# Batched matmul on one core: the small zeroing store beside the first loads writes 16 rows of 512 B instead of 128

## The chip, the cores and the metric

The kernel runs on one core of a Trainium2 chip (trn2). The metric is device microseconds of that core, as the median of several executions. Lower is better.

Engines in the profile: PE is TensorE (matmul), PEld its weight loads, DVE is VectorE, ACT is ScalarE, POOL is GpSimd, SP is SyncE. "SPq" and "ACTq" are the two queues on which this kernel starts DMAs. In this kernel SBUF holds the tiles of a, b and the output, PSUM is what the matmuls write to, and an eviction copies a result from PSUM to SBUF. "Packet records" are the lines that the packed trace keeps for each DMA packet: its start, duration, size and queue. They don't name the DMA engine, so a time "per engine" below is a sum divided by 16, unless the text says otherwise. In this kernel a data packet is one row (6144 packets of 8192 B for 48 full transfers of 128 rows). The records also hold 4-byte packets, 16 for each full transfer, here read as the semaphore writes that report completion, one for each engine that a transfer uses: each of the first four casts of before starts 0.36 to 0.43 us after the last of the 16 of its load. The load rows agree with 16 engines: 128 rows of 309 ns pass in 2.45 us, so 16 run at a time.

## The reference

```python
# batch 16, K = M = N = 512, float32
def reference(a, b):            # a: [16, 512, 512] (k, m), b: [16, 512, 512] (k, n)
    return np.matmul(a.transpose(0, 2, 1), b).astype(np.float32)
```

It reads 32 MiB and writes 16 MiB. That traffic sets most of the kernel's time, as the profile below shows.

## The kernel before

Each batch has two loads of 1 MiB (a and b), two casts to bf16 on DVE, 16 matmuls on PE, two evictions from PSUM on ACT and one store of 1 MiB. SP issues all loads and then all full stores. The output of every batch has its own SBUF tile, so no store has to make room for anything. A full load or store has 128 rows of 8192 B.

```python
    with tc.tile_critical(no_gpsimd_drain=True):
        def load(i):
            j = i % NL                                    # NL = 3 load buffers
            if i >= NL:
                nc.sync.wait_ge(s_acast, i - NL + 2)
            nc.sync.dma_start(a_ts[j][:], a_v[i]).then_inc(s_a[j], 16)
            nc.sync.dma_start(b_ts[j][:], b_v[i]).then_inc(s_b[j], 16)

        def store(i):
            if i == 0:
                nc.sync.wait_ge(s_w, 16)                  # the small store has landed
            nc.sync.wait_ge(s_ev1, i + 1)
            nc.sync.dma_start(out_v[i], o_ts[i][:]).then_inc(s_o, 16)

        for i in range(batch):
            load(i)
        for i in range(batch):
            store(i)
        nc.sync.wait_ge(s_o, 16 * batch)
        # ... DVE: wait for a, cast; wait for b, cast.  PE: 16 matmuls a batch (cut)

        nc.gpsimd.memset(o_ts[0][:, 0, 0:P], 0.0).then_inc(s_z, 1)
        nc.scalar.wait_ge(s_z, 1)
        nc.scalar.dma_start(out_v[0][:, 0, 0:P], o_ts[0][:, 0, 0:P]).then_inc(s_w, 16)
        nc.scalar.wait_ge(s_w, 16)
        for i in range(batch):
            for h in range(H):                            # H = 2
                nc.scalar.wait_ge(s_mm, H * i + h + 1)
                nc.scalar.copy(
                    out=o_ts[i][:, 2 * h:2 * h + 2, :], in_=ps_ts[(i % NB) * H + h][:]
                ).then_inc(s_ev1 if h else s_ev0, 1)
```

The last block is the subject. Before any matmul has finished, POOL zeroes 128 rows x 128 columns of the first output tile and ACT stores them. The full store of batch 0 overwrites the bytes later, so the result doesn't need this store. ACT waits for the store to land before its first eviction, because that eviction overwrites the tile that the store reads.

## Time and profile before

| | before |
|---|---|
| time, median of 3 | 125.76 us (125.68 to 125.79) |
| span of the profiled execution | 123.6 us |
| PE / DVE / ACT busy | 48% / 32% / 27% |
| DMA engines | 9 tenths or more in all but the first and last of 40 slices |

From the page of the kernel before: the DMA rows of the 40 slices (share of time the 16 DMA engines are busy, then GB/s), the packets, the two queues, and the issues with their time from issue to landing.

```profile
DMA  2999999999999999999999999999999999999993
GB/s 58 414 424 430 424 424 424 424 419 424 424 424 422 416 424 422 422 424 424 419 414 422 422 424 424 424 422 427 424 427 427 432 430 424 427 435 427 427 424 143
DMA packets 7056, 50.40 MB, mean 408 GB/s; under 512 B 784, under 2 KB 912, under 8 KB 912
...
q1 hardware_dynamic: 6912, 50.33, 97.6%
q10 hardware_dynamic: 144, 0.07, 0.2%
...
a<-in_a_dram SPq DMA_DIRECT2D x16, 1024.0 KB, 8.6
...
out_dram<-o ACTq DMA_DIRECT2D x1, 64.0 KB, 4.9
```

The 9s say that the DMA engines have work from the second slice to the last but one. This kernel ends when its DMA stream ends: from 100 to 118 us there is no compute at all, and the DMA share is 1.01. q1 is SP's queue, q10 ACT's: 144 packets, 128 rows and 16 semaphore writes. The 784 packets under 512 B are the 4-byte ones: 16 for each of 48 full transfers, and 16 for the small store, so by the reading above each DMA uses all 16 engines.

From the timeline of the kernel before (start us, duration us, engine, line, operation; in brackets the idle time before it and what ended it):

```profile
0.94 0.38 SPq L63 DMA_DIRECT2D a<-in_a_dram  x1
0.94 0.20 POOL L108 MEMSET o<- 128x128 f32 x1 [0.50 <-SPq L57]
1.18 0.37 ACTq L110 DMA_DIRECT2D out_dram<-o  x1
...
5.98 1.23 DVE L83 CAST abf<-a 128x2048 bf16<-128x2048 f32 x1 [5.98 <-DMA a<-in_a_dram]
8.51 1.23 DVE L85 CAST bbf<-b 128x2048 bf16<-128x2048 f32 x1 [1.31 <-DMA b<-in_b_dram]
11.01 1.23 DVE L83 CAST abf<-a 128x2048 bf16<-128x2048 f32 x1 [1.27 <-DMA a<-in_a_dram]
...
13.70 1.28 ACT L115 ACT_TABLE_LOAD   x1 [13.70 <-PE ps L97]
...
88.28 1.01 ACT L115 COPY o<-ps 128x1024 f32<-128x1024 f32 x1 [0.71 <-PE ps L97]
```

The casts start when their loads land, so their starts are a clock of the DMA stream. ACT's store is issued at 1.18 us and lands 4.9 us later, at about 6.1 us. ACT has nothing to do until 13.7 us anyway, and its release there comes from PE. The last eviction ends at 89.3 us; the remaining 34 us are stores draining.

### The profile page before, as it was taken

What the parts mean: (1) busy time and instruction counts of PE and PEld (TensorE: products, weight loads), DVE (VectorE), ACT (ScalarE), POOL (GpSimd) and SP (SyncE); (2) the same over time, 40 slices, a digit from 0 to 9 for tenths busy, and PEclk for the clock granted to TensorE, in tenths of its full rate; (3) what the DMA queues carried; (4) which work ended last, traced back from release to release, by engine and by line L of the source; (5) the groups of instructions that cost most, each with busy time, mean ns of one, the idle gap of its engine ahead of it and who ended that gap; (6) DMA issues with size and microseconds to landing.
All of it is one profiled execution on the core that took longest, in us unless ns stands there. A gap on an engine that the chain in (4) does not pass through costs nothing. (4 is left out here: it accounts for less than half of the span.)

```text
span 123.6 us, 750 instructions
## 1 busy us (share of the span) xinstructions
PE 59.6 (48%) x256; PEld 28.0 (23%) x256; DVE 39.3 (32%) x32; ACT 33.6 (27%) x33; POOL 0.4 (0%) x5
## 2 busy tenths in 40 slices
PE   0007979695865956859659578596500000000000
PEld 0002344252332522424325234243200000000000
DVE  0055345633554356435543464352000000000000
ACT  0000565623425336244263352432600000000000
POOL 1000000000000000000000000000000000000000
PEclk9999999999999999999999999999985555555555
DMA  2999999999999999999999999999999999999993
GB/s 58 414 424 430 424 424 424 424 419 424 424 424 422 416 424 422 422 424 424 419 414 422 422 424 424 424 422 427 424 427 427 432 430 424 427 435 427 427 424 143
DMA packets 7056, 50.40 MB, mean 408 GB/s; under 512 B 784, under 2 KB 912, under 8 KB 912
## 3 DMA queue, kind: packets, MB, share of 16 engines
q1 hardware_dynamic: 6912, 50.33, 97.6%
q10 hardware_dynamic: 144, 0.07, 0.2%
HBM read 33.55 MB, written 16.84 MB: 408 GB/s over the span
## 5 line engine op out<-in xcount | busy, mean ns | idle before, releaser
L97 PE MATMUL ps<-bbf,abf 128*128 128x512 bf16 x256 | 59.6, 387 | 28.7 <-PEq L94 28.7
L115 ACT COPY o<-ps 128x1024 f32<-128x1024 f32 x32 | 32.3, 1013 | 42.0 <-PE ps L97 42.0
L97 PEld LDWEIGHTS ps<-bbf,abf 128*128 128x128 bf16 x256 | 28.0, 114 | 59.8 <-issue 37.6
L83 DVE CAST abf<-a 128x2048 bf16<-128x2048 f32 x16 | 19.6, 1227 | 25.8 <-DMA a<-in_a_dram 25.8
L85 DVE CAST bbf<-b 128x2048 bf16<-128x2048 f32 x16 | 19.6, 1227 | 19.3 <-DMA b<-in_b_dram 19.3
L115 ACT ACT_TABLE_LOAD x1 | 1.3, 1283 | 13.7 <-PE ps L97 13.7
L108 POOL MEMSET o<- 128x128 f32 x1 | 0.2, 205 | 0.5 <-SPq L57 0.5
L132 POOL MEMSET const-bfloat16-1.0<- 128x1 bf16 x1 | 0.1, 102 | 0.0
L132 POOL MEMSET const-uint8-127<- 128x1 uint8 x1 | 0.1, 102 | 0.0
L132 POOL MEMSET const-float32-0.0<- 128x1 f32 x1 | 0.1, 99 | 0.2 <-issue 0.2
L132 POOL MEMSET const-float32-1.0<- 128x1 f32 x1 | 0.1, 99 | 0.0
## 6 DMA issues: line engine op xcount, KB each, us to landing
a<-in_a_dram SPq DMA_DIRECT2D x16, 1024.0 KB, 8.6
b<-in_b_dram SPq DMA_DIRECT2D x16, 1024.0 KB, 10.7
out_dram<-o SPq DMA_DIRECT2D x16, 1024.0 KB, 25.8
out_dram<-o ACTq DMA_DIRECT2D x1, 64.0 KB, 4.9
```

The lines of the kernel that those rows point to most:

```text
L83: nc.vector.tensor_copy(out=abf_ts[i % NB][:], in_=a_ts[i % NL][:]).then_inc(s_acast, 1)
L85: nc.vector.tensor_copy(out=bbf_ts[i % NB][:], in_=b_ts[i % NL][:]).then_inc(s_bcast, 1)
L97: mm = nc.tensor.matmul(ps_ts[u * H + mo // 2][:, mo % 2, :], a_m[:, ko, mo, :], bbf_ts[u][:, ko, :], start=(ko == 0), stop=(ko == KO - 1),)
L108: nc.gpsimd.memset(o_ts[0][:, 0, 0:P], 0.0).then_inc(s_z, 1)
L115: nc.scalar.copy(out=o_ts[i][:, 2 * h:2 * h + 2, :], in_=ps_ts[(i % NB) * H + h][:]).then_inc(s_ev1 if h else s_ev0, 1)
L132: nc = _bacc.Bacc("TRN2", target_bir_lowering=False, num_devices=1)
```

## The change

The intent is to make the small store smaller: one eighth of the rows.

```diff
-        nc.gpsimd.memset(o_ts[0][:, 0, 0:P], 0.0).then_inc(s_z, 1)
+        nc.gpsimd.memset(o_ts[0][0:16, 0, 0:P], 0.0).then_inc(s_z, 1)
         nc.scalar.wait_ge(s_z, 1)
-        nc.scalar.dma_start(out_v[0][:, 0, 0:P], o_ts[0][:, 0, 0:P]).then_inc(s_w, 16)
+        nc.scalar.dma_start(out_v[0][0:16, 0, 0:P], o_ts[0][0:16, 0, 0:P]).then_inc(s_w, 16)
         nc.scalar.wait_ge(s_w, 16)
```

## The prediction

> **What bounds the kernel.** The DMA engines. In the page's 40 slices the DMA row is at 9 tenths from the second slice to the last but one, at 414 to 435 GB/s. The queue table gives the SP queue, with all loads and all full stores (50.33 MB), 97.6% of the 16 engines' span of 123.6 us. PE is busy 48%, DVE 32%, ACT 27%. The chain of waits ends in the last eviction, at 89.3 us; after it run only stores queued long before: from 100 to 118 us there is no compute and DMA share 1.01. The SP queue's own waits (57.9 us for DVE's casts) don't matter: about two loads are always queued. So only DMA engine time, or the ramp of the first 3 us, can move the total.
>
> **What the change removes.** The zeroing store on the ACT queue goes from 128 rows of 512 B to 16. In the trace's packet records that queue has 128 data packets of 27 ns and 16 semaphore packets of 9 ns: 3.60 us of engine time, 0.225 us for each of the 16 engines (the 0.2% of the queue table). After: 16 x 27 + 16 x 9 = 0.58 us, 0.036 us each. Saved: 0.19 us per engine. [...] I expect one data packet per engine. The memset (0.20 us on POOL) shrinks too. The order of instructions is unchanged on every engine, and nothing is added.
>
> **How much is on the critical path.** Nearly all. [...] the small store's packets run 2.6 to 3.7 us after the first load packet, when the engines are already fed, and the first b lands 2.58 us after the first a where later loads are 2.45 us apart: 0.12 us more; the rest of the 0.22 us falls into the first a. Every later packet is shifted by it, to the end. ACT's wait for the small store (landing 4.9 us after issue, at about 6.1 us) costs nothing: ACT's first work starts at 13.7 us, released by PE.
>
> **Prediction.** 125.76 - 0.19 = 125.57 us, with 8 in 10 between 125.25 and 125.90. Faster by over 2%: 1%; within 2%: 98%; slower by over 2%: 1%.
>
> **What would show each step.** (1) ACT queue: 32 packets instead of 144, under 0.05% of the engines' span; 6944 packets in all. (2) The interval from first a to first b falls from 2.58 towards 2.46 us. (3) Casts, matmuls, evictions and stores start about 0.2 us earlier, with unchanged durations; first cast at about 5.85 instead of 5.98 us. (4) The span falls to about 123.4 us. (5) The small store's landing falls from 4.9 to about 4.2 us. (6) Load packets keep their mean (about 313 ns in mid-run, against 309 ns for stores).
>
> **What would make it wrong.** Load packets take 309 ns in the first 10 us and 313 ns between 20 and 80 us. If that depends on the engines' relative phase, and the small store sets that phase, the 4096 load packets could gain or lose up to about 4 ns each: 1.1 us in all, more than the saving and of either sign. If the small store mostly filled time in which the engines would have waited in the ramp, the gain would be nearer zero. Both stay far inside 2%.

The sum: 0.225 us per engine before, 0.036 us after, 0.19 us saved. 16 rows going to 16 engines, one data packet each: the 0.036 us rest on that, and the trace of before could not show it.

## The result, and the profile after

Ratios here are the mean time of one kernel's runs over that of the other's of the same rounds, so they are not quite the ratio of the medians that are quoted.

| | before | after |
|---|---|---|
| time, median of 6 | 125.78 us (125.68 to 125.85) | 125.57 us (125.50 to 125.61) |
| ratio to before, 95% interval | | 0.9983, [0.9970, 0.9996] |
| span of the profiled execution | 123.6 us | 123.5 us |

The change saves 0.21 us by the medians. The same lines of the page, after:

```profile
DMA  3999999999999999999999999999999999999993
GB/s 53 417 435 427 427 422 425 422 419 419 425 425 425 425 425 425 422 419 419 422 422 417 419 425 425 422 425 427 425 425 430 433 425 430 433 425 427 425 425 130
DMA packets 6944, 50.34 MB, mean 408 GB/s; under 512 B 784, under 2 KB 800, under 8 KB 800
...
q1 hardware_dynamic: 6912, 50.33, 97.8%
q10 hardware_dynamic: 32, 0.01, 0.0%
...
out_dram<-o ACTq DMA_DIRECT2D x1, 8.0 KB, 4.3
```

The DMA row has the same shape, 112 packets are gone, and the 784 packets under 512 B are still 784. In the packet records of after each of the 16 rows starts 3 to 4 ns before a load row ends, and a load row starts 23 to 24 ns after it, another one for each small row: 16 rows still use 16 engines. The timeline after:

```profile
0.95 0.19 POOL L108 MEMSET o<- 16x128 f32 x1 [0.50 <-SPq L57]
1.17 0.38 ACTq L110 DMA_DIRECT2D out_dram<-o  x1
...
5.80 1.23 DVE L83 CAST abf<-a 128x2048 bf16<-128x2048 f32 x1 [5.80 <-DMA a<-in_a_dram]
8.27 1.23 DVE L85 CAST bbf<-b 128x2048 bf16<-128x2048 f32 x1 [1.24 <-DMA b<-in_b_dram]
10.75 1.23 DVE L83 CAST abf<-a 128x2048 bf16<-128x2048 f32 x1 [1.25 <-DMA a<-in_a_dram]
...
88.00 1.01 ACT L115 COPY o<-ps 128x1024 f32<-128x1024 f32 x1 [0.71 <-PE ps L97]
```

The first cast starts 0.18 us earlier, the second 0.24 us, the third 0.26 us, and the last eviction 0.28 us. So the shift arises in the first two loads and is then carried along. In the packet records of the two traces the last packet of the SP queue ends 119.94 us after the first one before, and 119.74 us after the change: 0.19 us less. The spans differ by only about 0.1 us. One pair of profiles can't be read finer than that: the profiled execution of before was at 125.61 us itself one of the fastest of its kernel. The packet records also show how the 128 rows of before run: by their spacing, the first three of each engine's eight rows alternate with load rows (329 to 330 ns apart), and the other five come in one burst, 23 to 30 ns apart, between the last row of the first a and the first row of the first b. The interval from first a to first b, 2.58 us with them and 2.45 us without, shows the burst: 5 x 23.5 ns = 0.12 us.

### The profile page after: what moved, and what is told of

It reads as the page before. It is cut to its first block, busy times and chain, and to the rows that moved or that the text cites. A ratio compares the mean times of both kernels' runs of the same rounds, so it can differ in the third digit from the quotient of the medians.

```text
span 123.5 us, 750 instructions
## 1 busy us (share of the span) xinstructions
PE 60.3 (49%) x256; PEld 28.1 (23%) x256; DVE 39.3 (32%) x32; ACT 33.7 (27%) x33; POOL 0.4 (0%) x5
## 2 busy tenths in 40 slices
DMA packets 6944, 50.34 MB, mean 408 GB/s; under 512 B 784, under 2 KB 800, under 8 KB 800
## 5 line engine op out<-in xcount | busy, mean ns | idle before, releaser
L97 PE MATMUL ps<-bbf,abf 128*128 128x512 bf16 x256 | 60.3, 390 | 27.7 <-PEq L94 27.6
```

Source lines behind the costliest of these rows:

```text
L97: mm = nc.tensor.matmul(ps_ts[u * H + mo // 2][:, mo % 2, :], a_m[:, ko, mo, :], bbf_ts[u][:, ko, :], start=(ko == 0), stop=(ko == KO - 1),)
```

## The experiments

Theory A was the prediction's: the DMA engines are always busy, so each packet of the small store pushes the whole stream back by its own length. Rivals were a fixed cost per DMA (B), a useful phase of the engines (C), the release of ACT (D), and a cost that only the start-up has (E). Each kernel was timed in 5 rounds against before (4 to 6 executions of each). Twelve runs were made, all with the right result. "Difference" is the difference of the medians from before in the same rounds. The interval of each small ratio is about 0.0013 to either side, that is 0.16 us.

| run | what it has | time us | before us | ratio | difference us |
|---|---|---|---|---|---|
| e1_none | no small store | 125.47 | 125.82 | 0.9969 | -0.35 |
| e2_no_act_wait | 128 rows, ACT doesn't wait | 125.80 | 125.82 | 0.9999 | -0.02 |
| e3_mid_run | 128 rows, amid the loads | 125.59 | 125.82 | 0.9982 | -0.23 |
| e4_x8_128rows | 8 stores of 128 rows | 133.32 | 125.82 | 1.0569 | +7.50 |
| e5_127rows | 127 rows | 138.58 | 125.81 | 1.1016 | +12.77 |
| e6_wide | 128 rows of 2048 B | 126.33 | 125.81 | 1.0047 | +0.52 |
| e7_memset_full | store 16 rows, zero 128 | 125.45 | 125.81 | 0.9968 | -0.36 |
| e8_x8_16rows | 8 stores of 16 rows | 125.57 | 125.81 | 0.9981 | -0.24 |
| e9_x8_no_wait | as e4, ACT doesn't wait | 126.93 | 125.69 | 1.0095 | +1.24 |
| e10_127_no_wait | as e5, ACT doesn't wait | 128.11 | 125.69 | 1.0191 | +2.42 |
| e11_x8_mid | 8 stores of 128 rows, amid the loads | 126.52 | 125.69 | 1.0069 | +0.83 |
| e12_after_again | the changed kernel | 125.36 | 125.69 | 0.9974 | -0.33 |

### e1_none: no small store

```diff
-            if i == 0:
-                nc.sync.wait_ge(s_w, 16)
...
-        nc.gpsimd.memset(o_ts[0][:, 0, 0:P], 0.0).then_inc(s_z, 1)
-        nc.scalar.wait_ge(s_z, 1)
-        nc.scalar.dma_start(out_v[0][:, 0, 0:P], o_ts[0][:, 0, 0:P]).then_inc(s_w, 16)
-        nc.scalar.wait_ge(s_w, 16)
```

> No small store, no memset for it, no waits for it. Theory A (DMA engine time: every packet of the small store delays the saturated stream by its own length): 0.225 us below before, about 125.55 us, and only 0.036 us below the changed kernel. Rival B (the small store has a fixed cost as a DMA, beside its rows, that 16 rows still pay): clearly more than 0.225 us below before. Rival C (the small store sets a useful phase of the engines): no gain, or a loss, and load packets of another mean than 313.5 ns in mid-run.

It took 125.47 us, 0.35 us below before, interval of the ratio [0.9956, 0.9982]. The upper end is 0.23 us below before, about where theory A's 0.225 us stands, so the size is at the edge of what A allows. Rival C falls: there is a gain, and the load packets in mid-run have the same mean (313.5 ns) as in both kernels. Rival B is not settled by this run.

### e2_no_act_wait: all 128 rows, but ACT doesn't wait

```diff
+    z_t = pool.tile([P, P], f32, name="z0")
...
-        nc.gpsimd.memset(o_ts[0][:, 0, 0:P], 0.0).then_inc(s_z, 1)
+        nc.gpsimd.memset(z_t[:], 0.0).then_inc(s_z, 1)
         nc.scalar.wait_ge(s_z, 1)
-        nc.scalar.dma_start(out_v[0][:, 0, 0:P], o_ts[0][:, 0, 0:P]).then_inc(s_w, 16)
-        nc.scalar.wait_ge(s_w, 16)
+        nc.scalar.dma_start(out_v[0][:, 0, 0:P], z_t[:]).then_inc(s_w, 16)
```

> All 128 rows stay, but the source is a tile of its own and ACT no longer waits for the store; the wait before the first full store stays on SP. Theory A: same as before within 0.06 us, since the engines move the same packets. Rival D (the smaller store helped because ACT, or the compute behind it, is released earlier): near the changed kernel, about 0.2 us below before.

125.80 us, ratio 0.9999: nothing gained. With one small store ACT's wait is free, and rival D falls as an explanation of the change.

### e7_memset_full: half of the change alone

```diff
-        nc.gpsimd.memset(o_ts[0][0:16, 0, 0:P], 0.0).then_inc(s_z, 1)
+        nc.gpsimd.memset(o_ts[0][:, 0, 0:P], 0.0).then_inc(s_z, 1)
```

(against the changed kernel)

> The store of 16 rows as in the changed kernel, but the memset of all 128 rows as before: half of the change alone. Theory A: the time of the changed kernel, 0.19 to 0.2 us below before. If the memset carried any of the gain: nearer before.

125.45 us, 0.36 us below before. The whole gain is there without the smaller memset: the store's rows carry it.

### e12_after_again: the changed kernel once more

> The changed kernel once more, in the same rounds as these. It was 0.21 us below before; with the memset of all rows it was 0.36, with no store 0.35. If those differ only by noise: 0.2 to 0.36 below before, so 125.45 to 125.6. It shows how far such differences can be read.

125.36 us, 0.33 us below before. (The time is just under the expected 125.45 us because before itself was 0.12 us lower in these rounds than in the earlier ones; the difference lies in the expected range.) So three comparisons of a 16-row store with before gave 0.21, 0.36 and 0.33 us, mean 0.30 us. A difference of 0.1 us between two of these runs says nothing.

### e4_x8_128rows: eight stores at the start

```diff
-        nc.scalar.dma_start(out_v[0][:, 0, 0:P], o_ts[0][:, 0, 0:P]).then_inc(s_w, 16)
-        nc.scalar.wait_ge(s_w, 16)
+        for c in range(8):
+            nc.scalar.dma_start(
+                out_v[0][:, c // 4, (c % 4) * P:(c % 4 + 1) * P], o_ts[0][:, 0, 0:P]
+            ).then_inc(s_w, 16)
+        nc.scalar.wait_ge(s_w, 128)
```

(SP's wait before the first full store goes to 128 as well.)

> Eight small stores of 128 rows of 512 B at the start instead of one. Theory A: 7 x 0.225 = 1.58 us above before, about 127.35 us (1.25% slower), with 1152 packets of 3.6 us x 8 engine time on the ACT queue. A rival by which the rows only fill a gap of the ramp, or by which rows write in parallel with the loads' HBM reads (packets' durations overlap): clearly less, under 0.8 us.

It cost 7.50 us instead of 1.58. The page shows at once that this is another mechanism (DMA rows of the 40 slices of e4_x8_128rows):

```profile
DMA  3999999980399999999999999999999999999993
GB/s 52 416 421 423 421 418 421 421 354 0 85 429 424 424 434 419 424 421 416 429 421 424 419 421 426 419 426 421 421 436 429 424 424 436 424 426 429 429 426 140
```

The DMA engines, which never pause in before, stand still for more than a slice (a slice is 3.3 us). The waits of the same run (engine, line, who was waited for, us in total, times, longest) name who held them up:

```profile
DVE abf L83 <- PE ps L97: 14.1, 3, 11.9
ACT o L118 <- DMA out_dram<-o: 9.6, 1, 9.6
```

Neither line is among before's waits. ACT waits 9.6 us for the small stores before it evicts anything. PE then has no free PSUM (it starts again at 26.2 us, once the evictions have begun at 25.0), so DVE may not overwrite the bf16 tiles (the first line), so SP may not issue the next loads (it waits for a cast of a for up to 14.9 us, where before had 8.0), and the DMA queue runs dry. The small stores land so late (25.0 us from the start of the span) because their rows don't go first: in the packet records most 512 B rows come one load row apart (their 64 rows per engine are spread over 20 us).

### e5_127rows: one row less

```diff
-        nc.gpsimd.memset(o_ts[0][:, 0, 0:P], 0.0).then_inc(s_z, 1)
+        nc.gpsimd.memset(o_ts[0][0:127, 0, 0:P], 0.0).then_inc(s_z, 1)
         nc.scalar.wait_ge(s_z, 1)
-        nc.scalar.dma_start(out_v[0][:, 0, 0:P], o_ts[0][:, 0, 0:P]).then_inc(s_w, 16)
+        nc.scalar.dma_start(out_v[0][0:127, 0, 0:P], o_ts[0][0:127, 0, 0:P]).then_inc(s_w, 16)
```

> 127 rows instead of 128: one row less, 512 B less. [...] Theory A, read by the engine (the engine with the most work sets the end): 127 x 27 ns = 3.43 us on that one engine against 0.225 us, so about 3.2 us above before, 129.0 us (2.5% slower), and all 127 data packets run one after the other. If it is the bytes or the packets in all that count: the same as before within 0.05 us. If the later loads can be taken up by the 15 others: in between[...].

Two passages are cut: the reason given for all 127 rows going to one engine, and a claim about whether later loads could move to the other engines. No run had shown either by then, so the 3.2 us rested on an assumption of the author. This run shows the first; e10 shows one engine still at work 2.45 us after all others.

It cost 12.77 us. One row fewer makes the kernel 10% slower. Two lines of the page of e5_127rows, and one of its waits:

```profile
DMA  3999999900039999999999999999999999999993
...
DMA packets 7040, 50.40 MB, mean 369 GB/s; under 512 B 769, under 2 KB 896, under 8 KB 896
```

```profile
ACT o L115 <- DMA out_dram<-o: 15.6, 1, 15.6
```

769 packets under 512 B are the 768 of the full transfers and a single one for the small store: 127 rows ran on one engine. The stretch from 28 to 30 us, when the queued loads are through, agrees: its DMA share is 0.06, one engine of 16. In the packet records the 512 B rows come 329 to 330 ns apart for most of 26 us, which fits one load row of 309 ns before each. The exceptions are a burst of eight rows between the first a and the first b, and one row more at each later change from one load to the next. The store landed at 31.1 us, about 30 us after its issue (before's 128 rows took 4.9 us), and ACT's first eviction waited for it. My expectation had only the engine time in it. The run therefore mixes two effects, and so does e4; e9 and e10 take them apart.

### e9_x8_no_wait and e10_127_no_wait: the same stores without ACT's wait

Both store from a tile of their own, so ACT needs no wait. For eight stores:

```diff
+    z_t = pool.tile([P, P], f32, name="z0")
...
-        nc.gpsimd.memset(o_ts[0][:, 0, 0:P], 0.0).then_inc(s_z, 1)
+        nc.gpsimd.memset(z_t[:], 0.0).then_inc(s_z, 1)
         nc.scalar.wait_ge(s_z, 1)
-        nc.scalar.dma_start(out_v[0][:, 0, 0:P], o_ts[0][:, 0, 0:P]).then_inc(s_w, 16)
-        nc.scalar.wait_ge(s_w, 16)
+        for c in range(8):
+            nc.scalar.dma_start(
+                out_v[0][:, c // 4, (c % 4) * P:(c % 4 + 1) * P], z_t[:]
+            ).then_inc(s_w, 16)
```

(SP's wait before the first full store goes to 128.)

> Eight stores of 128 rows at the start as in the run that cost 7.5 us, but from a tile of their own and without ACT's wait for them, so that evictions never wait. Theory A' (engine time alone; a 512 B packet lengthens the stream by its start-to-start distance of 23.5 ns, which the records of the 127-row run show, and the rest of the 7.5 us was ACT waiting): 7 x 8 x 23.5 ns = 1.3 us, up to 1.6 us with 225 ns each, above before: 127.1 to 127.4 us, and no stretch with an idle DMA row. If the DMA engines themselves stall on many small writes: still some 7 us above before.

For 127 rows it is the edit of e2 with `z_t[0:127, :]`:

> 127 rows from a tile of its own, without ACT's wait. Theory A': the one engine that has all 127 packets gets 127 x 23.5 ns = 2.98 us more work, the others none, and the slowest engine sets the end: 2.98 - 0.19 = 2.8 us above before, about 128.6 us. If bytes in all count: 125.6 to 125.8 us. If the DMA stall of the earlier run was not ACT's wait: 12 us above before again.

Eight stores now cost 1.24 us, so ACT's wait was about 6.3 us of e4's 7.5. The 127 rows cost 2.42 us, so the wait was about 10.4 us of e5's 12.8. The small remainders are what theory A is about. Both came out below the 1.3 to 1.6 us and the 2.8 us that had been expected. In e9 no slice is idle any more, as expected (DMA row of e9_x8_no_wait):

```profile
DMA  4999999999999999999999999999999999999993
```

In e10 the end of the run shows one engine working alone (stretches of the trace from:to, length, busy time of the engines, granted clock, DMA share, GB/s):

```profile
120.00:121.00 1.00, 0.00 (x0) 0.00 (x0) 0.00 (x0) 0.00 (x0) 0.00 (x0) 0.50 1.00 426
121.00:122.00 1.00, 0.00 (x0) 0.00 (x0) 0.00 (x0) 0.00 (x0) 0.00 (x0) 0.50 0.39 164
122.00:123.00 1.00, 0.00 (x0) 0.00 (x0) 0.00 (x0) 0.00 (x0) 0.00 (x0) 0.50 0.08 33
123.00:124.00 1.00, 0.00 (x0) 0.00 (x0) 0.00 (x0) 0.00 (x0) 0.00 (x0) 0.50 0.06 25
```

A share of 0.06 is one engine of 16. Fifteen engines are done near 121.5 us, and the sixteenth, by inference the one that carried the rows, needs about 3 us more. In the packet records its last semaphore write comes 2.87 us after the mean of the other fifteen, and 2.45 us after the last of them: 127 rows of 23.5 ns would be 2.98 us. In before the engines end up to 0.37 us apart, and it is the slowest of them that the run is compared with; that may be part of why the run cost less than 2.8 us. So in this run the engine with the most work set the end, and the bytes in all did not.

### e3_mid_run and e11_x8_mid: the same rows later

e3 takes the block at the start away (as e1 does, but SP's wait stays) and adds after the evictions of batch 6:

```diff
+            if i == 6:
+                nc.scalar.wait_ge(s_ev1, 1)
+                nc.scalar.dma_start(out_v[0][:, 2, 0:P], o_ts[0][:, 2, 0:P]).then_inc(s_w, 16)
```

> The store of 128 rows of 512 B is taken from the start and issued by ACT after its evictions of batch 6, amid full loads, with finished values. Theory A: engine time costs the same anywhere in a saturated stretch, so same as before within 0.06 us. Rival E (the rows cost time because they sit in the start-up, where everything later waits for the first a and b): about the time of the changed kernel or less, 0.2 us below before.

125.59 us, 0.23 us below before, interval of the ratio [0.9969, 0.9995]. Theory A as stated had expected no difference, within 0.06 us. The interval excludes zero; its end, at 0.06 us below before, just touches what A had allowed. e11 magnifies it: one such store after each of the batches 4 to 11, writing the finished values of eight different pieces of the first output tile (SP waits for 128).

> Eight stores of 128 rows, one after each of the batches 4 to 11, nothing at the start. Theory A': the same as eight at the start without the wait, 127.1 to 127.4 us, 1.5 to 1.8 us above no store at all. If the time of rows in mid-run is partly free (as 125.59 us for one store in mid-run against 125.81 for it at the start hints), it is clearly less, by 0.1 us for each store: about 126.3 to 126.5 us. If it is the start-up alone that costs 0.2 us once, whatever the number: 0.2 us below eight at the start.

It took 126.52 us, 0.83 us above before. Against no store at all (0.35 us below before) eight stores in mid-run cost 1.18 us, 0.15 us each; eight at the start (e9) cost 1.59 us, 0.20 us each. So rows in mid-run are not free, but cheaper. The packet records show a refund: in e11 the load packets between which the rows come last 309.8 ns, where they last 313.5 ns otherwise. Summed over the 3840 load packets after the first 256, each engine's load packets took 0.48 us less than in e1_none, which is 0.06 us for each small store. In the start-up, once the ramp's first 2.6 us are over, load packets last 309 ns anyway. But e9 gets a refund too, later: in before the load packets lengthen to about 313 ns from about 15 us after the first packet on, in e9 they stay at 309.0 ns until about 32 us, some 10 us after its last small row. That makes 0.26 us per engine less than in e1_none, 0.03 us for each store. So the refund accounts for 0.22 us of the 0.41 us between e9 and e11, and the rest is not much more than the interval of one comparison. Why load packets have these two lengths, and what ends the short ones, no run shows.

### e8_x8_16rows: as many rows in eight issues

```diff
-        nc.scalar.dma_start(out_v[0][0:16, 0, 0:P], o_ts[0][0:16, 0, 0:P]).then_inc(s_w, 16)
-        nc.scalar.wait_ge(s_w, 16)
+        for c in range(8):
+            nc.scalar.dma_start(
+                out_v[0][0:16, c // 4, (c % 4) * P:(c % 4 + 1) * P], o_ts[0][0:16, 0, 0:P]
+            ).then_inc(s_w, 16)
+        nc.scalar.wait_ge(s_w, 128)
```

(against the changed kernel; SP waits for 128 too)

> Eight stores of 16 rows of 512 B: as many data packets as before's one store of 128 rows, but eight issues and 128 semaphore packets. Theory A: 8 x (27 + 9) = 0.288 us per engine, so 0.06 us above before and 0.25 us above the changed kernel. Rival B (each DMA has a fixed cost to the stream, beyond its packets): 7 x that cost above; with 0.1 us each, 0.7 us above before.

125.57 us, 0.24 us below before, where 0.06 us above had been expected. Rival B falls clearly, since eight issues cost no more than one. But the number of theory A is missed too: by packets e8 has slightly more engine time than before (4.61 us against 3.60 us on the ACT queue) and is yet faster. Two things differ. Its rows are spread over 7 us instead of 1.1 us. And its load packets stay at 309 ns until about 18 us after the first packet, where those of before lengthen from about 15 us on; this saves 0.08 us per engine, about a quarter of the 0.30 us by which the expectation missed.

### e6_wide: longer rows

```diff
-        nc.gpsimd.memset(o_ts[0][:, 0, 0:P], 0.0).then_inc(s_z, 1)
+        nc.gpsimd.memset(o_ts[0][:, 0, 0:N], 0.0).then_inc(s_z, 1)
         nc.scalar.wait_ge(s_z, 1)
-        nc.scalar.dma_start(out_v[0][:, 0, 0:P], o_ts[0][:, 0, 0:P]).then_inc(s_w, 16)
+        nc.scalar.dma_start(out_v[0][:, 0, 0:N], o_ts[0][:, 0, 0:N]).then_inc(s_w, 16)
```

> 128 rows of 2048 B instead of 512 B: four times the bytes in as many packets. Theory A with time by bytes (8192 B take 309 ns, 512 B take 27 ns, so about 8 ns + 0.0367 ns per B: 83 ns for 2048 B): 8 x 56 = 0.45 us above before, 126.2 us. If a packet's cost is fixed, not its bytes: same as before. The memset of 128x512 is longer, which A says costs nothing.

126.33 us, 0.52 us above before, where 0.45 had been expected. In the packet records each of these rows takes 84 ns, against 27 ns for a row of 512 B. Four times the bytes in as many packets cost what the bytes need, so the cost is the time for which the rows hold the engines, and not the number of packets alone.

## Why the prediction was right

The predicted time was 125.57 us and the measured median was 125.57 us. The mechanism is the predicted one, but that the number fits to the hundredth is luck: two later comparisons of a 16-row store gave 0.36 and 0.33 us instead of 0.21, and the first comparison's interval alone reaches from 0.05 to 0.38 us. Point by point:

- **DMA bounds the kernel: right.** Adding engine time added run time (0.52 us in e6, 1.24 in e9, 0.83 in e11), on one engine as well (2.42 us in e10). Removing a wait of ACT added or saved nothing (e2: 0.02 us below before), nor did the larger memset (e7: 0.36 us below before, where the changed kernel was 0.21 and 0.33 below).
- **ACT's DMA takes engine time from SP's: right.** In the packet records of after each of the 16 small rows runs between two load rows, whose starts are 329 to 337 ns apart there, against 305 to 306 ns three rows later. The records place the semaphore writes of the first a and the first b 2.58 us apart with 128 rows and 2.45 us with 16, as predicted in point 2.
- **The marks.** 32 packets and 6944 in all: right. The first cast was expected at about 5.85 us and came at 5.80. The store's landing was expected at about 4.2 us after issue and took 4.3. The mean of the load packets is unchanged at 313.5 ns. The span fell by 0.1 us in the one pair of profiles, half of what was expected, and the timed runs fell by 0.21 us.
- **The size is less exact than it looks.** I took 27 ns for each row. In e5's records rows without a load row between them start 23.5 ns apart, so the seven rows that each engine is spared are worth 0.165 us by that distance, instead of 0.19. The times with many rows give, against e1_none, 1.59 us / 64 rows = 25 ns a row and engine at the start (e9), 1.18 / 64 = 18 ns in mid-run (e11), and 2.77 / 127 = 22 ns on one engine (e10). Against these, the mean of 0.30 us for the change's seven rows is 43 ns a row.
- **What stays open.** The one burst of 128 rows in the start-up seems to cost about 0.1 us more than its packets. Two things speak for it: e3 and e8 have about as much engine time in small rows as before and are 0.23 and 0.24 us faster; and the first b's semaphore writes come, in the mean, 6.04 and 6.11 us after the first packet in the two traces with 128 rows, against 5.83 to 5.84 us in the three with 16, a difference of 0.24 us where packets explain 0.165. The surplus lies before the first a has landed, and there three traces without a store at the start scatter by 0.17 us among themselves (3.27 to 3.44 us). No run isolates it, and it is smaller than one comparison's interval of 0.16 us.
- **The doubts.** The fear that the small store sets a phase of the engines, worth up to 1.1 us, did not come true for this change: summed, the load packets take the same 75.12 us per engine in both kernels. A smaller relative of it did in the experiments: load packets shorten to 309.8 ns while small rows run between them (e11), and with more or longer-spread small rows at the start the 309 ns load packets went on until about 18 us (e8) and 32 us (e9), instead of 15 us.
- **"ACT's wait for the small store costs nothing": right here, but not robust.** The store landed 7.6 us before ACT needed it (6.1 against 13.7 us). In e5 most rows on an engine put the landing off by about 0.33 us each while loads are queued, because they alternate with load rows. With 64 rows an engine (e4, landing at 25.0 us) or 127 on one (e5, at 31.1 us) the margin is gone.

The fastest versions are those without the store or with 16 rows: 125.47 us and 125.36 to 125.57 us. These runs can't tell them apart. Since the result doesn't need the store, leaving it out is the simplest.

## What to carry to other kernels

Where the DMA row is full from end to end, the worth of removing a small transfer can be estimated beforehand: its rows per engine, times the time that a row holds an engine. Here that gave 0.165 to 0.19 us, where 0.21 to 0.36 us were measured; effects of 0.1 us in the ramp or in the length of the load packets stay outside the estimate. Everything else about it, the issue, the memset, the landing, was free here as long as nobody waited for it: eight issues of 16 rows were 0.24 us below before, the larger memset with 16 rows 0.36 us, and taking ACT's wait away changed 0.02 us. But check who waits: beside the deep queue of loads the small transfers here landed late, mostly row by row between load rows (at 25.0 us with 64 rows an engine), and 127 rows ran on one engine and landed at 31.1 us. ACT's wait, harmless in before with a margin of 7.6 us, then stopped the whole pipeline: it was worth about 6.3 us of e4's 7.5 and 10.4 us of e5's 12.8.
